# Measured TensorE and ScalarE durations in the build-time clock of a two-layer hybrid decoder kernel

## Chip, cores and metric

The kernel runs on one core of a Trainium2 chip as one program. The metric is the device time of one execution in microseconds (us), as the median over executions. The engines of the core are named as in the profile: PE (TensorE matmuls), PEld (its weight loads), DVE (VectorE), ACT (ScalarE), POOL (GpSimd) and SP (SyncE, which issues the DMAs here).

## What is computed

Two layers, each of three sub-layers in a row: a SwiGLU feed-forward network (FFN) at half weight, a token mixer, and a second such FFN. Each sub-layer is wrapped in RMS norms before and after it and in a shift, a scale and a gate that come from a conditioning vector `c`. The sequence has 256 rows, the model 1024 columns, the FFN 2816; all data are float32.

```python
def swiglu(h, w_in, w_out):
    gate, up = jnp.split(h @ w_in, 2, axis=-1)
    return (jax.nn.silu(gate) * up) @ w_out

def token_mixer(h, ...):
    proj = h @ w_in
    u, q, k, v, f, g_a, g_b = jnp.split(proj, cuts, axis=-1)
    y_ssm = s5_ssm(u, a_re, a_im, log_dt, b_re, b_im, c_re, c_im, d_skip)
    z_val, z_gate = jnp.split(jax.nn.gelu(y_ssm) @ glu_w, 2, axis=-1)
    y_a = z_val * jax.nn.sigmoid(z_gate)
    attn = forgetting_attention(q.reshape(shp), k.reshape(shp), v.reshape(shp), f + forget_b)
    y_b = attn @ attn_w_out
    merged = jax.nn.sigmoid(g_a) * y_a + jax.nn.sigmoid(g_b) * y_b
    return merged @ w_out

def reference(...):
    for l in range(DEPTH):
        mod = (jax.nn.silu(c) @ mod_w[l] + mod_b[l]).reshape(bsz, N_SUB, 3, D_MODEL)
        def pre(x_in, i):
            return rms_norm(x_in, norm_pre[l, i]) * (1.0 + mod[:, i, 1]) + mod[:, i, 0]
        def post_add(x_in, y, i, res_w):
            return x_in + res_w * mod[:, i, 2] * rms_norm(y, norm_post[l, i])
        x = post_add(x, swiglu(pre(x, 0), ffn_w_in[l, 0], ffn_w_out[l, 0]), 0, FFN_RES)
        y = token_mixer(pre(x, 1), ...)
        x = post_add(x, y, 1, 1.0)
        x = post_add(x, swiglu(pre(x, 2), ffn_w_in[l, 1], ffn_w_out[l, 1]), 2, FFN_RES)
    return x
```

`s5_ssm` is a diagonal state-space model with complex states (32 groups of 16 channels, 64 states each), and `forgetting_attention` is causal softmax attention with 8 heads of 64 and a bias that is a running sum of log-sigmoids.

## The kernel before

**Weights.** All weights come as one stream of pieces of 128 x 1024 float32, in an order worked out ahead. A product is made of three matmuls in the float32r type, of a high and a low part of both operands: `hi` with `xh`, `hi` with `xl`, `lo` with `xh`. So each piece goes through four steps: a DMA into a tile `raw`, a copy on ACT into `hi`, a subtraction on DVE into `lo`, and matmuls on PE. A piece of the modulation weights (`mod_w`) goes through a DMA and one DVE instruction (`raw<-raw,crow`), which sums into a column of `mc`; when the eight pieces of a vector are in, it is put to use, and after three gates PE transposes their columns (`gT`) so that they can be laid out as rows.

**Rows in two halves.** The 256 rows are two halves of 128. At a sub-layer's end, a half goes from its product `y` through `yg` (times a row of gates), `x` (added to the stream), `xn` (normalised), the PE transposes `xt<-kc,xn`, ACT's `xh<-xt,mc` and DVE's `xl<-xt,mc,xh`, and is then input to the next sub-layer. While the second half passes this chain, PE does the next sub-layer's first products for the first half alone: `n` in an FFN (natural orientation, turned around later with `hn`), `v` and `ga0` in a mixer. The function `pre_split` (line 555) issues the transposes of a half, and `hook` (line 1877) decides at which matmul.

**A mixer.** In this order PE does `v` and `ga0` (half of the first gate), `q`, `k`, `u`, then `ga1`, `gb0`, `gb1` (the rest of the gates). Each takes four pieces; `gb0_0` to `gb0_3` are the four pieces of `gb0`, and so on. Between them stand the attention: `sc<-kt,qt` (scores), on DVE `lg<-nbd,cq,sc` and `st<-lg` (bias, maximum), on ACT the exponentials `lg<-lg,st`, on PE the transposes `sc<-kc,lg`, on ACT their copy `lg<-sc`, on PE `sc<-lg,v` (values), then `ath` and `atl`, the parts of the result. `nbd` are masks of the bias. The state-space branch has tables that depend on the parameters alone (`pw`, `wc`, `ws`, `wt`: powers; `bt`, `bpr`, `bpi`: input matrices; `bT`, `D`, `cd`: transposed tables and the direct term) and work on data: `U` (copies of `u`), `vr`/`vi` on PE, products and scans on DVE that end in `zr` and `zi`, on PE `ys<-U,d` and `ys<-zr,c`. Behind them come `yb` (attention output, times the gate into `gb`), the copies `yg<-g` in pairs of one on DVE and one on ACT, `ygh` and `ygl` (parts of the branch's result), `z`, the merge `mt` and `ym` (the mixer's output).

**What sets the order.** The program is straight-line: the order of instructions is made when it is built. Each engine call goes through `Timed`, which tells a `Plan` what was issued; the plan keeps a clock for each engine, adds what `cost` (line 183) gives, and knows so when each tile would be ready. The PE's instructions are issued by plain loops; everything else waits in generators (`Task`, `Part`) with ranks. After each PE instruction `pace` lets `pick` (line 223) issue what could start by the PE's clock:

```python
            at = max(at, self.clk[eng])
            if t.rank <= 0:
                soon[eng] = min(at, soon.get(eng, at))
            elif soon.get(eng, 1e9) < max(at, now) + HOLD:
                continue
            at = max(at, now)
            if at <= until and (best is None or at < best[0]):
                best = at, t
```

The order on DVE and ACT, the DMAs (a DMA is issued when a tile of the stream comes free), and some of PE's order follow from this. On PE it is `hook`, which issues transposes once the clock has passed the chain's end,

```python
            if not last and not (task.done and task.at <= self.plan.clk["pe"]):
                return
```

and in the mixer `fill`, `past` and `there`, which put weight matmuls between the steps of the attention and the state-space branch until these are ready by the clock. The clock is a number in the builder only; the chip waits on semaphores, so another order changes no result. The constants that go with the clock (`HOLD`, `TURN`, `SLACK`, `KEPT`, `TABLES` and others at the top of the file) stay as they are.

Of the kernel before, what the change touches and what calls it, by code (L numbers as in the profile page):

```python
# [10 lines left out]
F32R = mybir.dt.float32r  # L11
# [152 lines left out]
class Plan:  # L164
# [18 lines left out]
    def cost(self, eng, op, outs, aps):  # L183
        n = max(x.free_size() for x in (outs or aps))
        if eng == "pe":
            if op == "transpose":
                return 0.107
            r = aps[-1]
            c = r.free_size() / 2400
            return max(c, 0.107) if r.dtype == F32R else max(4 * c, 0.214)  # L190
        if eng == "dve":
            return 0.07 + n / 960
        if eng == "act":
            return (0.1 if len(aps) < 3 else 0.18) + n / 1200
        if eng == "pool":
            return 0.4 + n / 400
        return n * 4 * P / 360e3
# [1763 lines left out]
```

## Time and profile before

| | us |
|---|---|
| three executions | 1183.67, 1193.74, 1189.22 |
| their median | 1189.22 |
| the profiled execution | 1182.35 |
| span of its trace, first to last instruction | 1180.6 |
| mean granted PE clock | 0.992 |
| PE idle for `z` waiting for `ygh`, once | 4.8 |
| PE idle for `gT` waiting for `mc`, once | 2.8 |
| PE idle for `v` waiting for `xl`, three times in all | 3.1 |

The span is one execution on the chip; the profiled execution's own time has 1.75 us more, which lie outside the first and last instruction. Times in the trace are microseconds from the span's start. A row of the timeline has the start, the length, the engine, the line, the operation with out<-in, and, in brackets, how long the engine idled before it and what released it. PE is pipelined: a 512-column matmul is listed with 0.39 us, while the next starts 0.23 us after it.

### The profile page before, as it was taken

To read this page: it belongs to the slowest core of one execution; us is meant where nothing else is said; L and a number is where in the kernel's file an instruction comes from. 1 tells how busy PE (TensorE), PEld (TensorE's weight loads), DVE (VectorE), ACT (ScalarE), POOL (GpSimd) and SP (SyncE) were. 2 spreads that over 40 slices of the span, in tenths; PEclk is the share of its full clock that TensorE was granted. 3 is DMA by queue.
4 is the path that set the end of the run, shared out by engine and by line. 5 is a ranking of instruction groups with operands and counts; after the bars stand their busy time and mean duration, and the time that the engine had idled before them with its cause. 6 is when DMAs were issued, how large, how long until landed. Compare 5 with 4: busy or idle time off the path is not lost.

```text
span 1180.6 us, 19407 instructions
## 1 busy us (share of the span) xinstructions
PE 1140.6 (97%) x7488; PEld 1015.5 (86%) x7488; DVE 912.7 (77%) x1529; ACT 608.6 (52%) x943; POOL 36.2 (3%) x62
## 2 busy tenths in 40 slices
PE   8999999998998999999999999999999999999997
PEld 5999998796786779999979989987987887999995
DVE  6988987897998889999678878878448798855532
ACT  5653452685556564444364475356355756543421
POOL 1000000000000010000010000001000001000000
PEclk9999999998999999999999999999999999999999
DMA  9999887577887669999769398966645566765300
GB/s 361 408 367 407 301 286 267 187 257 236 339 306 249 224 235 390 360 376 381 246 214 355 127 330 284 373 248 237 227 127 179 180 212 216 284 224 204 126 19 36
DMA packets 99186, 306.50 MB, mean 260 GB/s; under 512 B 16373, under 2 KB 26133, under 8 KB 99094
## 3 DMA queue, kind: packets, MB, share of 16 engines
q1 hardware_dynamic: 99094, 305.27, 71.6%
q8 instruction: 58, 0.95, 0.3%
q14 instruction: 34, 0.28, 0.1%
HBM read 291.51 MB, written 13.71 MB: 259 GB/s over the span
## 4 chain that ended last, share of the span: by engine, by line
PE 86%; DVE 7%; ACT 3%; DMA 2%; issue 2%; POOL 1%; SPq 0%; DVEq 0%; POOLq 0%; ACTq 0%
PE f L128 35%; PE y L128 20%; PE n L128 5%; PE ym L128 3%; PE ga L128 3%; PE gb L128 3%; PE z L128 3%; PE k L128 2%; PE q L128 2%; PE v L128 2%; PE ys L128 2%; PE u L128 2%; ACT xh L128 1%; DVE raw L128 1%; PE yb L128 1%
## 5 line engine op out<-in xcount | busy, mean ns | idle before, releaser
L128 DVE TENSOR_TENSOR lo<-raw,hi 128x1024 fp32r<-128x1024 f32 x368 | 437.1, 1218 | 27.2 <-ACT hi L128 21.3
L128 ACT ACTIVATE hi<-raw 128x1024 fp32r<-128x1024 f32 x367 | 370.7, 1055 | 68.3 <-PE f L128 38.7
L128 PE MATMUL f<-xl,hi 128*128 128x256 f32 x1216 | 341.4, 281 | 2.7 <-DVE xl L128 2.7
L128 PE MATMUL f<-xh,hi 128*128 128x256 f32 x1216 | 342.0, 281 | 1.9 <-ACT xh L128 1.9
L128 PE MATMUL f<-xh,lo 128*128 128x256 f32 x1216 | 341.0, 280 | 0.0
L128 PEld LDWEIGHTS f<-xh,lo 128*128 128x128 f32 x1216 | 232.4, 191 | 0.0
L128 PEld LDWEIGHTS f<-xl,hi 128*128 128x128 f32 x1216 | 228.4, 188 | 4.6 <-DVE xl L128 3.6
L128 PEld LDWEIGHTS f<-xh,hi 128*128 128x128 f32 x1216 | 228.5, 188 | 3.8 <-ACT xh L128 2.5
L128 PE MATMUL y<-hi,ht 128*128 128x512 f32 x704 | 196.2, 391 | 0.8 <-DVE yg L128 0.8
L128 DVE SCALAR_TENSOR_TENSOR raw<-raw,crow 128x1024 f32<-128x1024 f32 x144 | 173.3, 1218 | 6.0 <-DMA raw<-ws 5.9
L128 PEld LDWEIGHTS y<-hi,ht 128*128 128x128 f32 x704 | 129.3, 188 | 26.2 <-DVE yg L128 1.1
L128 ACT ACTIVATE sg<-f 128x512 f32<-128x512 f32 x38 | 22.7, 597 | 222.7 <-PE f L128 215.4
L128 PE MATMUL y<-lo,ht 128*128 128x512 f32 x352 | 109.3, 390 | 0.8 <-ACT yg L128 0.8
L128 DVE TENSOR_TENSOR sg<-sg,f 128x512 f32<-128x512 f32 x38 | 26.1, 687 | 90.0 <-ACT sg L128 89.9
L128 PEld LDWEIGHTS y<-lo,ht 128*128 128x128 f32 x352 | 66.1, 188 | 15.1 <-ACT yg L128 1.2
L128 PE MATMUL n<-hi,xl 128*128 128x512 f32 x96 | 37.9, 395 | 1.7 <-DVE xl L128 1.7
L128 ACT ACTIVATE lg<-lg,st 128x128 f32<-128x128 f32 (+1 forms) x64 | 26.1, 444 | 25.3 <-DVE st L128 25.3
L128 PE MATMUL n<-hi,xh 128*128 128x512 f32 x96 | 38.4, 400 | 0.0
L128 PE MATMUL n<-lo,xh 128*128 128x512 f32 x96 | 37.7, 392 | 0.0
L128 DVE TENSOR_TENSOR yg<-y,row 128x1024 f32<-128x1024 f32 (+1 forms) x9 | 9.9, 1103 | 32.8 <-ACT xn L128 23.6
L128 DVE TENSOR_TENSOR ht<-sg,ht 128x512 fp32r<-128x512 f32 x38 | 26.1, 687 | 9.8 <-ACT ht L128 9.5
L128 ACT ACTIVATE xh<-xt,mc 128x128 fp32r<-128x128 f32 x80 | 21.7, 383 | 22.1 <-PE xt L128 22.1
(276 smaller groups left out, 1646.7 us busy)
## 6 DMA issues: line engine op xcount, KB each, us to landing
raw<-ws SPq DMA_DIRECT2D x512, 512.0 KB, 5.8
row<-sg SPq DMA_DIRECT2D x11, 512.0 KB, 8.0
sbt<-bT SPq DMA_DIRECT2D x8, 512.0 KB, 3.0
sc<-cd SPq DMA_DIRECT2D x16, 256.0 KB, 8.0
bt<-sbt SPq DMA_DIRECT2D x8, 512.0 KB, 4.5
c<-sc SPq DMA_DIRECT2D x8, 512.0 KB, 10.2
d<-sd SPq DMA_DIRECT2D x4, 512.0 KB, 4.6
w<-sw SPq DMA_DIRECT2D x4, 512.0 KB, 5.8
```

The costliest lines, as they stand in the source:

```text
L128: r = f(*a, **k)
```

## The change

The change is to the numbers in `Plan.cost` alone.

```diff
         if eng == "pe":
             if op == "transpose":
-                return 0.107
+                return 0.109
             r = aps[-1]
             c = r.free_size() / 2400
-            return max(c, 0.107) if r.dtype == F32R else max(4 * c, 0.214)
+            return c + 0.012 if r.dtype == F32R else max(4 * c, 0.224)
         if eng == "dve":
             return 0.07 + n / 960
         if eng == "act":
-            return (0.1 if len(aps) < 3 else 0.18) + n / 1200
+            return (0.19 if len(aps) < 3 else 0.27) + n / 1350
```

In the clock a 512-column float32r matmul now takes 0.225 us (0.213 before), one of 256 columns 0.119 (0.107), a small float32 one 0.224 (0.214), an ACT instruction on 1024 columns 0.949 (0.953) and one on 128 columns 0.285 (0.207). DVE's numbers stay: 1.137 us for 1024 columns. PE's clock so runs 6 to 11% slower against DVE's. The instructions are the same ones, on every engine; their order differs from the first pieces of the first FFN on.

PE, the start of the second FFN of layer 0, where `n` is made for the first half and the transposes of the second half come in. Before (`hi_4394` and `lo_4464` are the third piece, `hi_4404` and `lo_4495` the fourth):

```order
L128 MATMUL n_668_4504<-hi_4386,xl 128x512
L128 MATMUL n_668_4504<-hi_4394,xh 128x512
L128 MATMUL n_668_4504<-lo_4464,xh 128x512
...
L128 MATMUL n_668_4504<-hi_4394,xl 128x512
L128 MATMUL xt_4531<-kc,xn_635_4335 128x128 x8
L128 MATMUL n_668_4504<-hi_4404,xh 128x512
```

And now (`hi_4393` and `lo_4476` are the third piece):

```order
L128 MATMUL n_669_4506<-hi_4382,xl 128x512
L128 MATMUL xt_4525<-kc,xn_635_4335 128x128 x8
L128 MATMUL n_669_4506<-hi_4393,xh 128x512
L128 MATMUL n_669_4506<-lo_4476,xh 128x512
L128 MATMUL n_669_4506<-hi_4393,xl 128x512
...
L128 MATMUL n_669_4506<-hi_4402,xh 128x512
```

The eight transposes have moved ahead of the six matmuls of the third piece (three kinds, each for two blocks of 128 input columns; `hook` is called after each piece). The same move is made at five places: at the start of three FFNs like this one (the second of layer 0 and both of layer 1) and at the starts of both mixers, among the pieces of `ga0`. The first half's transposes move at one place only, at the start of the layer-0 mixer, from behind the last piece of the FFN to twelve matmuls ahead of that.

DVE, the layer-0 mixer around the first softmax. Before (`lo_3359` is the split of piece `ga1_2`):

```order
L128 TENSOR_TENSOR nbd_451_3110<-nbd_451_3110,cm 128x1024
L128 COPY U_3281<-u_3063 32x4x64
L128 SCALAR_TENSOR_TENSOR lg_3292<-nbd_449_3108,cq_3051,sc_3282 128x128
...
L128 TENSOR_REDUCE st_3293<-lg_3292 128x2 x2
L128 TENSOR_SCALAR st_3293<-st_3293 128x4
L128 COPY U_3281<-u_3063 32x4x64
L128 TENSOR_TENSOR wt_3237<-ws_3236,pw_3238 128x32
L128 TENSOR_TENSOR pw_3238<-pw_3238 128x16 x2
L128 TENSOR_TENSOR ws_3236<-wc_3235,pw_3238 128x16x2
L128 TENSOR_TENSOR pw_3238<-pw_3238 128x16 x2
L128 TENSOR_TENSOR lo_3359<-raw_424_2950,hi_3343 128x1024
```

And now (`lo_3427` is the split of piece `ga1_3`, `lo_3441` that of `gb0_0`):

```order
L128 TENSOR_TENSOR wt_3097<-ws_3096,pw_3098 128x512
L128 TENSOR_TENSOR wc_3095<-wc_3095,wt_3097 128x16x32
L128 COPY U_3339<-u_3179 32x4x64
L128 TENSOR_TENSOR nbd_461_3224<-nbp_3225,cm 128x1024
L128 TENSOR_TENSOR nbd_463_3226<-nbd_463_3226,cm 128x1024
L128 SCALAR_TENSOR_TENSOR lg_3350<-nbd_461_3224,cq_3177,sc_3340 128x128
...
L128 TENSOR_REDUCE st_3351<-lg_3350 128x2 x2
L128 TENSOR_SCALAR st_3351<-st_3351 128x4
L128 TENSOR_TENSOR lo_3427<-raw_419_2891,hi_3403 128x1024
L128 RECIPROCAL st_3351<-st_3351 128x4
L128 TENSOR_TENSOR lo_3441<-raw_422_2907,hi_3410 128x1024
```

The powers (`pw`, `wc`, `ws`, `wt`) were at 32 columns at this point and are now at 512, their last; the split of `ga1_2` now stands ahead of `nbd`, and the first split behind the softmax rows is that of the next piece, `ga1_3`. On PE `ga1_3` and `gb0_0` now stand ahead of the first transposes `sc<-kc,lg`, where they stood behind the state-space products `vr` and `vi`; all of `yb` for the first half stands ahead of `ys<-zr,c`, which had `yb` between its parts. On DVE the last two `gb<-gb,yb`, which follow the last `yb`, now stand ahead of all eight copies `yg<-g` of the branch's second half; three of these stood ahead of them.

PE, the end of the layer-0 mixer's `z`. Before:

```order
L128 MATMUL z_4173<-hi_4053,ygh_3871 128x512 x2
L128 MATMUL z_4173<-lo_4086,ygh_3871 128x512 x2
L128 MATMUL z_4173<-hi_4053,ygl_3872 128x512 x2
L128 MATMUL gT_4247<-kc,mc 24x128
L128 MATMUL ym_626_4256<-hi_4066,xh 128x512 x2
```

And now:

```order
L128 MATMUL z_4007<-hi_4038,ygh_3913 128x512 x2
L128 MATMUL z_4007<-lo_4058,ygh_3913 128x512 x2
L128 MATMUL z_4007<-hi_4038,ygl_3914 128x512 x2
L128 MATMUL gT_4146<-kc,mc 24x128
L128 MATMUL z_4151<-hi_4050,ygh_3913 128x512 x2
```

The transpose `gT` stood behind all of `z`, ahead of `ym`; it now stands in the middle of `z`, ahead of the second group of output columns. Its last modulation pieces on DVE stood behind `z` and now stand ahead of it.

In the layer-1 mixer, PE's first `ys<-zr,c` moves ahead of the last `sc<-lg,v` and the first piece of `yb`, and on ACT the copy `lg<-sc` of the third softmax moves ahead of one `hi`. In the FFNs the splits, the modulation pieces and the DMAs shift by some rows against PE.

## Prediction

> **What bounds the kernel now.** I read the page's busy shares first, then busy time by stage, then the waits of the tensor engine (PE), then the timeline at each long wait.
>
> ```profile
> span 1180.6 us, 19407 instructions
> PE 1140.6 (97%) x7488; PEld 1015.5 (86%) x7488; DVE 912.7 (77%) x1529; ACT 608.6 (52%) x943; POOL 36.2 (3%) x62
> ```
>
> ```profile
> 183.00:206.00 23.00, 23.00 (x108) 19.03 (x106) 17.13 (x23) 8.36 (x11) 1.59 (x4) 1.00 0.78 282
> 206.00:222.00 16.00, 13.29 (x60) 10.36 (x60) 11.02 (x18) 11.64 (x27) 2.35 (x4) 1.00 0.44 148
> 222.00:276.00 54.00, 54.00 (x463) 49.96 (x461) 50.59 (x107) 37.02 (x67) 0.00 (x0) 1.00 0.71 244
> 276.00:316.00 40.00, 33.73 (x200) 26.92 (x200) 33.45 (x117) 23.98 (x60) 1.16 (x2) 0.91 0.80 280
> 316.00:361.00 45.00, 42.74 (x260) 35.68 (x259) 41.31 (x58) 26.46 (x45) 0.00 (x0) 1.00 0.85 321
> 361.00:394.00 33.00, 25.41 (x110) 20.43 (x109) 30.12 (x43) 21.09 (x28) 0.00 (x0) 0.95 0.75 247
> 394.00:430.00 36.00, 35.95 (x169) 28.98 (x167) 29.43 (x36) 19.02 (x36) 5.55 (x8) 1.00 0.62 211
> 430.00:605.00 175.00, 174.25 (x1190) 161.42 (x1190) 147.45 (x204) 81.18 (x101) 2.36 (x4) 1.00 0.88 333
> ```
>
> The windows are cut where stages end (`u` of the layer-0 mixer at 276). The columns are window, length, then busy time and instructions of PE, weight load, VectorE (DVE), ScalarE (ACT), GpSimd, then granted PE clock, DMA share and GB/s. PE is busy 1140.6 of 1180.6 us, so an order of instructions cannot win more than some tens of us. In an FFN (430 to 605) it idles 0.75 us of 175: nothing is to be won there. The layer-0 mixer, 276 to 394, leaves 6.3 + 2.3 + 7.6 = 16 us idle, and DVE is busy 104.9 of those 118 us: that stretch runs at DVE's pace as much as at PE's. What is decided there decides the time.
>
> ```profile
> 280.00:287.00 7.00, 3.29 (x14) 2.17 (x12) 6.76 (x22) 4.66 (x15) 1.16 (x2) 0.90 0.59 176
> 287.00:294.00 7.00, 6.04 (x21) 4.63 (x23) 4.83 (x32) 4.14 (x7) 0.00 (x0) 0.62 0.69 228
> 367.00:374.00 7.00, 2.72 (x6) 2.15 (x7) 6.91 (x9) 6.06 (x8) 0.00 (x0) 0.78 0.86 268
> 905.00:910.00 5.00, 3.63 (x18) 2.82 (x19) 4.89 (x10) 2.38 (x3) 0.00 (x0) 0.68 0.61 211
> ```
>
> Here the granted clock falls behind waits. The lost clock is 7 x 0.10 + 7 x 0.38 = 3.4 us, 7 x 0.22 = 1.5 and 5 x 0.32 = 1.6: about 1.6 us for each cut, two of them around 287.
>
> **The change, part by part.** No instruction is added or removed, so all costs are waits. In the FFNs the order of weight splits shifts by a few rows; PE has no wait there and the splits keep their lead: 0, with 0 to +1 as bounds. The head, where PE waits for DVE,
>
> ```profile
> PE f L128 <- DVE xl L128: 2.7, 4, 0.9
> ```
>
> keeps DVE's rows but for swaps of neighbours: 0, and no more than one such wait of 0.9 either way.
>
> *Second-half transposes.* The transposes `xt` of rows 128 to 255 go six 512-column matmuls earlier at five places. One of them:
>
> ```profile
> 613.49 1.28 DVE L128 SCALAR_TENSOR_TENSOR xn<-x,ssx,row 128x1024 f32<-128x1024 f32 x1 [0.75 <-POOL ssx L128]
> ...
> 614.83 1.09 PE L128 MATMUL xt<-kc,xn 128*128 128x128 f32 x8
> ...
> 616.47 0.39 PE L128 MATMUL n<-hi,xh 128*128 128x512 f32 x1
> 616.70 0.39 PE L128 MATMUL n<-lo,xh 128*128 128x512 f32 x1
> ...
> 617.62 0.40 PE L128 MATMUL n<-lo,xh 128*128 128x512 f32 x1
> 618.58 0.50 PE L128 MATMUL n<-hi,xl 128*128 128x512 f32 x1 [0.56 <-DVE xl L128]
> ```
>
> ```profile
> PE n L128 <- DVE xl L128: 1.7, 3, 0.6
> ```
>
> `xn` ends at 614.77 and the transposes start 0.06 us behind it. In the new order DVE has the same rows ahead of `x` and `xn` (only the product `yg` goes ahead of one split, and `x` comes right where it came), so `xn` ends when it did, and PE meets the transposes 6 x 0.23 = 1.36 us too early. It gets back the wait behind them: 618.58 - 617.62 is 0.96 against a pitch of 0.23, so 0.73, and about 0.1 for the slower start after a wait. Net 1.36 - 0.84 = +0.52, three times by the row of waits; at the layer-1 mixer that wait is longer,
>
> ```profile
> 812.97 0.50 PE L128 MATMUL v<-hi,xl 128*128 128x512 f32 x1 [0.80 <-DVE xl L128]
> ```
>
> and +0.3 is left. Together +1.9; bounds 0 (if `xn` comes earlier with `yg`) and 4 x 1.36 = +5.4. The fifth place is the next part.
>
> *Boundary into the layer-0 mixer.* The first transposes go twelve matmuls (2.7 us) earlier, which hides a wait of 1.46 us behind them:
>
> ```profile
> 208.73 0.50 PE L128 MATMUL v<-hi,xl 128*128 128x512 f32 x1 [1.46 <-DVE xl L128]
> ```
>
> In their place eight table products of the state-space branch (0.3 to 1 us each) stand on DVE ahead of the splits of the third and fourth value pieces. Laid end to end from `xl`, DVE ends these splits at about 210.0 and 212.4, where PE wants them at 208.9 and 211.6; then `ga0_1` waits some 1.3 us. About 3 us of new waits against 1.9 + 1.1 us of old ones: 0, bounds -1.9 and +1.9.
>
> *Layer-0 mixer.* When `u` ends (276.0) DVE has done 6.4 us more of rows than before (the powers of the state matrix, less three modulation pieces and a split). DVE idled 5.9 + 5.0 + 3.4 = 14.3 us from 183 to 276, so these fit. Then:
>
> ```profile
> 277.68 1.20 DVE L128 TENSOR_TENSOR nbd<-nbp,cm 128x1024 f32<-128x1024 f32 x1
> ...
> 281.82 0.35 DVE L128 SCALAR_TENSOR_TENSOR lg<-nbd,cq,sc 128x128 f32<-128x128 f32 x1
> ...
> 283.38 1.00 DVE L128 TENSOR_REDUCE st<-lg 128x2 f32<-128x256 f32 x2
> ...
> 284.10 0.50 PE L128 MATMUL ga<-hi,xh 128*128 128x512 f32 x1 [1.43 <-ACT hi L128]
> ...
> 285.61 1.22 DVE L128 TENSOR_TENSOR lo<-raw,hi 128x1024 fp32r<-128x1024 f32 x1
> ...
> 286.88 0.79 PE L128 MATMUL ga<-lo,xh 128*128 128x512 f32 x1 [2.28 <-DVE lo L128]
> ```
>
> Before, `ga1_2` waits 1.43 + 2.28 us, since its split stands behind the softmax rows. Now its split comes ahead of them, and `ga1_3`, which PE meets next, takes its place. Ahead of the split of `ga1_3` DVE has, from 276: two `nbd` and two copies of `U` (281.82 - 277.68 = 4.1 us), two more copies and four table rows (by their columns, 1024 taking 1.2: 2 x 0.3 + 4 x 0.6 = 3.0), two splits (2.4), six `lg` (283.38 - 281.82 = 1.6), `st` (1.1) and itself (1.2): 13.4, so 289.4. PE, which would have begun `ga1_2` at about 284.1 - 1.5 = 282.6 and needs 12 x 0.23 = 2.7 us for it, is there at 285.3 and waits 4.1 us, with a clock cut behind it as at 287. I walked on in this way, DVE's rows laid end to end and PE's beside them. The softmax parts are now parted by weight pieces on PE, so that the smaller waits mostly go: of the 6.3 + 2.3 us idle until 361, 3.7 are those of `ga1_2` and some 4 of the rest. With the 3.4 us of clock PE wins 11 and pays 4.1: 7 us ahead. But DVE, which by then has been busy without a break, takes back half: the split of `gb1_3` comes 1.4 us late, and the first product of `yb` waits about 3 us, its `atl` standing behind two scan products; 1 us of old waits goes there. So `yb` ends about 3.5 us earlier. Then the second half of `z`:
>
> ```profile
> 361.40 1.28 DVE L128 SCALAR_TENSOR_TENSOR gb<-gb,yb 128x512 f32<-128x512 f32 x2
> ...
> 370.61 0.61 ACT L128 ACTIVATE ygh<-yg 128x512 fp32r<-128x512 f32 x1
> ...
> 371.28 1.22 PE L128 MATMUL z<-hi,ygh 128*128 128x512 f32 x2 [4.79 <-ACT ygh L128]
> ...
> 393.00 0.27 PE L128 MATMUL gT<-kc,mc 128*24 128x128 f32 x1 [2.81 <-DVE mc L128]
> ```
>
> Before, `ygh` starts 9.2 us after the `gb` products that follow `yb`, three of its eight copies on DVE, each in turn with one on ACT, being done ahead of them. Now all eight come behind, which at about 0.8 a pair makes 11.6. So `z` goes on 3.5 - 2.4 = 1.1 us earlier than at 371.3, after a wait of some 7 us that takes in the clock cut as before. The row transpose `gT` stands where its modulation rows are long done, so 2.8 us go. With +0.5 for a later `xl` and +1.5 for the clock cut behind `ga1_3`: -1.1 - 2.8 + 0.5 + 1.5 = -1.9. Bounds: all the idle time of 276 to 394 gone, -16; nothing gained and the 6.4 us of DVE rows late, +6.4. I take the walk's value, since the rows that make it are in the trace.
>
> *Layer-1 mixer.*
>
> ```profile
> 899.82 0.18 DVE L128 RECIPROCAL st<-st 128x4 f32<-128x4 f32 x1 [0.90 <-ACT lg L128]
> ...
> 906.37 1.21 PE L128 MATMUL sc<-lg,v 128*64 128x128 f32 x12 [1.85 <-ACT lg L128]
> ...
> 912.86 1.50 ACT L128 ACTIVATE lg<-lg,st 128x128 f32<-128x128 f32 x4
> ...
> 914.35 0.82 PE L128 MATMUL sc<-kc,lg 128*128 128x128 f32 x6
> ...
> 918.61 0.88 PE L128 MATMUL sc<-lg,v 128*64 128x128 f32 x12
> 918.85 1.22 DVE L128 TENSOR_TENSOR zr<-zr,t 128x1024 f32<-128x1024 f32 x1
> ```
>
> ACT's copy `lg<-sc` goes ahead of one split, so the wait of 1.85 shrinks by a split's 1.2, and the clock cut behind it (1.6) may go. But the next softmax, ready at 912.86 + 1.50 = 914.36, comes from DVE at its old time, and PE used it at 914.35: it now waits there for the 2.8 us it won. Behind that, `ys<-zr` stands ahead of the values; DVE saves the idle 0.90 at two reciprocals and ends `zr` 1.8 us earlier, about when PE comes; `atl`, behind copies of `yg`, costs some 0.5. Net +0.5, bounds -2.8 (both gains kept) and +2.5.
>
> Sum: +1.9 + 0 - 1.9 + 0.5 = +0.5 us on the profiled execution's 1182.35 us, so 1182.8. That execution lies 6.9 us under the median 1189.22 of the three runs shown; against the median the sum gives 1189.7 us.
>
> [...] By the rows, a wait of 1.85 us (906.37) was followed by a cut clock, one of 1.46 (208.73) was not (1.00 in 206 to 222), nor one of 2.81 (393.00; 1.00 in 394 to 430). [...]
>
> **The rivals.**
> Faster: DVE's rows pack better than in my walk, and of the 16 us idle and 5 us of lost clock in the layer-0 mixer half goes, 10.5 in place of 1.9: 1181; if all but 3 go, 1174. For it speaks that DVE has 13 us idle in 276 to 394; against it, that most of the waits there end on DVE's own chain of scans, products and copies, which grows no shorter.
> Slower, by the clock: the new waits of 1.4 to 1.6 us at four transposes, and those of about 3 us in both mixers, are each followed by a cut of 1.6: 6 x 1.6 = +9.6, 1199. It decides whether 1.6 us suffices; the rows leave that open between 1.46 and 1.85.
> Slower, by DVE: if the 6.4 us of earlier rows are not absorbed, the softmax and all behind it come that much later: +6.4, 1196; it decides if less than half of DVE's 14.3 idle us before 276 can be used, because rows stand behind one that waits.
> No effect at all, if the new numbers gave the old order, is excluded by the pieces of order shown above; its time would be 1189.
>
> **How the numbers follow.** Forecast 0.58, faster rival 0.18, clock 0.14, DVE 0.10. A measurement of this kernel can tell about 1% from no change, so the bounds are 1177.3 and 1201.1. Faster by over 1%: most of the faster rival and a tail of the forecast, 0.17. Slower: the slower rivals where both act or where the upper bounds of the transposes join them, 0.12. Within 1%: 0.71. The range, 1175 to 1199, takes in both slower rivals' values and most of the faster one's.
>
> **What would show it.** In the profile after: waits of `xt` for `xn` of about 1.5 us at four places and none of `n` for `xl` behind; no wait at `gT`; `ga<-lo` of about 4 us near 285 and `z<-ygh` of 7 us near 362; the wait at 906 small and one of 3 us before the next softmax transposes. The prediction is wrong if the FFNs get waits, if `f` waits longer for `xl` in the head, if `u` ends late because DVE's earlier rows did not fit, or if the clock is cut behind waits of 1.5 us.

## The result, and the profile after

The changed kernel takes 1224.43 us (median of 4 executions, 1221.38 to 1225.74), the kernel before on the same chip 1186.45 us: ratio 1.031, 95% interval 1.025 to 1.037. It is slower by about 3%, and the forecast was no change. The profiled execution took 1223.9 us. Its page begins, and has as busy time of the engines:

```profile
span 1222.1 us, 19426 instructions
...
PE 1160.6 (95%) x7488; PEld 1034.8 (85%) x7488; DVE 913.9 (75%) x1529; ACT 608.9 (50%) x943; POOL 34.7 (3%) x62
```

DVE and ACT have the work that they had, to 0.2%. PE has the same 7488 matmuls, yet was busy 20.0 us longer (1160.6 against 1140.6): they ran at a lower clock (0.971 granted in the mean over the execution, against 0.992). The other 21.5 us of the 41.5 are idle time. Where these arose is seen when both spans are cut at the same places in the work: the first matmul `n` of the second feed-forward (FFN) of layer 0, the first matmul of layer 1's `q`, and the first `n` of layer 1's second FFN. Windows of before and then of after; the columns are window, length, busy time and instructions of PE, PEld, DVE, ACT and POOL, granted PE clock, DMA share and GB/s:

```profile
0.00:417.10 417.10, 392.13 (x2556) 342.32 (x2557) 358.08 (x707) 234.85 (x383) 13.43 (x27) 0.99 0.83 300
417.10:826.40 409.30, 406.45 (x2725) 368.09 (x2724) 342.42 (x533) 210.56 (x305) 14.30 (x20) 1.00 0.80 297
826.40:985.00 158.60, 155.12 (x972) 134.62 (x971) 107.06 (x167) 87.16 (x157) 3.52 (x6) 0.99 0.58 191
985.00:1180.60 195.60, 186.90 (x1242) 170.51 (x1240) 105.16 (x125) 76.00 (x100) 4.95 (x9) 0.99 0.43 152
```

```profile
0.00:448.10 448.10, 406.62 (x2555) 355.24 (x2556) 359.26 (x707) 234.38 (x382) 15.23 (x27) 0.94 0.76 280
448.10:859.30 411.20, 405.67 (x2725) 367.82 (x2724) 342.25 (x534) 210.98 (x305) 11.81 (x20) 1.00 0.79 295
859.30:1026.20 166.90, 161.73 (x971) 141.17 (x970) 107.42 (x167) 86.85 (x156) 3.52 (x6) 0.95 0.52 182
1026.20:1222.10 195.90, 186.57 (x1242) 170.58 (x1240) 104.96 (x126) 76.67 (x100) 4.12 (x9) 0.99 0.43 151
```

The first stretch loses 31.0 us: idle time (length less PE's busy time) goes from 25.0 to 41.5, and busy time for the same matmuls from 392.1 to 406.6. The second, which is nearly all FFN, loses 1.9. The third, layer 1's mixer from `q` on, loses 8.3, of which 6.6 are busy time, the clock being 0.95 in place of 0.99. The last loses 0.3.

The 31.0 split further. The first transposes `xt` of layer 0's mixer begin 0.8 us later with twelve 512-column matmuls (2.7 us) fewer done, so 3.5 us were lost in the first FFN. When `u` begins the lag is 5.2 us (268.2 against 263.0), with 32 `D` matmuls more behind it; 16 of these took 0.66 us in a row, so the lag for the same work is 3.9, and the entry into the mixer cost 0.4. The other 27 us arise from `u` on in layer 0's mixer.

The 3.5 us at the head are a cut clock. Windows of before and of after:

```profile
20.00:30.00 10.00, 9.10 (x77) 8.91 (x78) 9.86 (x18) 6.47 (x11) 0.00 (x0) 1.00 1.03 406
```

```profile
20.00:30.00 10.00, 8.04 (x47) 7.84 (x48) 9.86 (x18) 6.25 (x10) 0.00 (x0) 0.66 1.03 408
```

PE's waits for `xl` are no longer in sum (2.5 us, before 2.7), but 1.96 of them now come in one piece, right behind a wait of 1.87 for `xh`, and the clock falls to 0.66: 47 matmuls in ten microseconds in place of 77. (In executions of kernels with the same start, below, `xt` begins between 203.0 and 205.9, so this part varies by some 3 us; before's own wait of 1.87 for `xh`, with one of 0.81 for `xl` behind it, left the clock at 1.00.)

**Layer 0's mixer.** The timeline of after, with what each instruction waited for in brackets:

```profile
290.99 2.95 ACT L128 ACTIVATE hi<-raw 128x1024 fp32r<-128x1024 f32 x3 [3.81 <-DMA snb<-cumt]
...
292.10 0.50 PE L128 MATMUL ga<-hi,xh 128*128 128x512 f32 x1 [2.28 <-ACT hi L128]
...
295.03 1.23 DVE L128 TENSOR_TENSOR nbd<-nbp,cm 128x1024 f32<-128x1024 f32 x1 [7.25 <-DMA nbp<-snb]
...
297.35 1.23 DVE L128 TENSOR_TENSOR nbd<-nbd,cm 128x1024 f32<-128x1024 f32 x1 [1.09 <-DMA nbd<-snb]
...
302.59 0.80 PE L128 MATMUL ga<-lo,xh 128*128 128x512 f32 x1 [9.99 <-DVE lo L128]
...
316.99 0.42 DVE L128 TENSOR_TENSOR atl<-sc,ath 128x256 fp32r<-128x256 f32 x1
...
317.51 0.66 PE L128 MATMUL vi<-U,bt 128*128 128x64 f32 x2 [3.53 <-issue]
```

PE stands 9.99 us before `ga1_3`'s `lo` matmuls. Its split is queued on DVE behind the masks `nbd`, and DVE itself stands 7.25 us for the transfer `nbp<-snb`. SP, which issues that transfer in its order, tells why. SP's issues in after, then in before (start, length of the issuing, what, how many):

```profile
267.05 12.56 SPq L128 DMA_DIRECT2D sd<-kt  x16
279.65 2.13 SPq L128 DMA_DIRECT2D bt<-sbt  x4
281.95 1.16 SPq L128 DMA_DIRECT2D d<-sd  x2
283.15 0.61 SPq L128 DMA_DIRECT2D snb<-cumt  x1
291.03 0.33 SPq L128 DMA_DIRECT2D nbp<-snb  x1
```

```profile
268.28 0.32 SPq L128 DMA_DIRECT2D snb<-cumt  x1
272.41 0.33 SPq L128 DMA_DIRECT2D nbp<-snb  x1
...
275.82 12.75 SPq L128 DMA_DIRECT2D sd<-kt  x16
288.62 1.86 SPq L128 DMA_DIRECT2D bt<-sbt  x4
```

In after, the state-space tables are done by the builder's clock before `u` is begun, since `D`'s last 32 matmuls have moved ahead; so their 16 stores `sd` and the loads `bt` and `d` go to SP ahead of `snb`. From `snb` to `nbp`, which needs it in memory, it then takes 7.9 us in place of 4.1, with the loads of `bt` and `d` under way. The masks are issued 18.6 us later than before, while `u` is only 5.2 us later.

The second stand, 3.53 us between the first `vr` and the first `vi` product, bears the releaser "issue": the profile sees no data that `vi` waits for. `atl` on DVE ends at 317.41 and `vi` starts at 317.51; `atl` reads the PSUM tile that `vi` is to overwrite, and now stands behind the six `lg` and the `st` of the next softmax. What follows it costs more than the stand. Windows of after:

```profile
318.00:326.00 8.00, 8.00 (x39) 8.00 (x39) 6.22 (x10) 2.48 (x9) 2.03 (x2) 0.50 1.03 408
326.00:334.00 8.00, 8.00 (x35) 7.61 (x35) 0.00 (x0) 1.65 (x2) 0.00 (x0) 0.50 0.94 358
334.00:342.00 8.00, 8.00 (x46) 5.79 (x46) 6.37 (x12) 1.44 (x3) 0.00 (x0) 0.97 0.30 101
```

PE is busy every moment from 318 to 334, at a clock of 0.50: a pair of `vr` and `vi` products (128x64, float32, each listed as two matmuls) takes 0.86 us, against 0.45 in before.

**Layer 1's mixer.** PE at the next softmax transposes, and the windows behind:

```profile
947.62 0.33 PE L128 MATMUL sc<-kc,lg 128*128 128x128 f32 x1 [2.54 <-ACT lg L128]
```

```profile
947.00:952.00 5.00, 4.02 (x21) 3.75 (x21) 4.97 (x6) 4.84 (x8) 0.00 (x0) 0.69 0.08 34
952.00:960.00 8.00, 8.00 (x39) 8.00 (x39) 5.44 (x5) 1.43 (x2) 0.00 (x0) 0.50 0.00 1
960.00:964.00 4.00, 4.00 (x26) 3.76 (x25) 0.52 (x2) 0.60 (x1) 0.00 (x0) 0.50 0.07 11
```

The same picture: a stand of 2.54 us, and then the narrow `ys` products run at 0.50 for some 14 us.

### The profile page after: what moved, and what is told of

It is laid out like the page before. It is cut to its first block, busy times and chain, and to the rows that moved or that the text cites. A ratio compares the mean times of both kernels' runs of the same rounds, so it can differ in the third digit from the quotient of the medians.

```text
span 1222.1 us, 19426 instructions
## 1 busy us (share of the span) xinstructions
PE 1160.6 (95%) x7488; PEld 1034.8 (85%) x7488; DVE 913.9 (75%) x1529; ACT 608.9 (50%) x943; POOL 34.7 (3%) x62
## 4 chain that ended last, share of the span: by engine, by line
PE 59%; DVE 4%; ACT 2%; issue 1%; POOL 1%; DMA 1%; DVEq 0%; POOLq 0%; ACTq 0%
PE f L128 25%; PE y L128 13%; PE n L128 4%; PE z L128 3%; PE ym L128 3%; PE ga L128 2%; PE ys L128 1%; PE gb L128 1%; PE yb L128 1%; PE u L128 1%; PE q L128 1%; PE k L128 1%; POOL ssx L128 1%; ACT xh L128 1%; PE xt L128 1%
## 5 line engine op out<-in xcount | busy, mean ns | idle before, releaser
L128 PE MATMUL ga<-lo,xh 128*128 128x512 f32 x64 | 26.3, 411 | 11.3 <-DVE lo L128 11.3
```

What stands on the lines that cost most here:

```text
L128: r = f(*a, **k)
```

## The experiments

Ratios are against the kernel before, run on the same chip; a difference to the changed kernel is one of medians (1224.4). The changed kernel was measured against other executions of before (1186.45), so such a difference is good to some 3 us only: by the ratios the gains of experiments 1, 2, 3, 6 and 7 are about 5, 4, 4, 4 and 23 us, and the intervals of the first four overlap the changed kernel's. What each edit does at its place is read from the traces.

**1. The three issues on another queue.** On the changed kernel, `snb`, `nbp` and `nbd` are issued by GpSimd (`side`):

```diff
+        self.side = Timed(plan, "dma", nc.gpsimd)
...
-        nc.sync.dma_start(row, ct[0:16, 0:P])
+        nc.side.dma_start(row, ct[0:16, 0:P])
...
-        nc.sync.dma_start(self.nb[1], flat[0:1, :].to_broadcast([P, D]))
-        nc.sync.dma_start(self.nb[2], flat[1:2, :].to_broadcast([P, D]))
+        nc.side.dma_start(self.nb[1], flat[0:1, :].to_broadcast([P, D]))
+        nc.side.dma_start(self.nb[2], flat[1:2, :].to_broadcast([P, D]))
```

> Of the changed kernel, with the three small transfers of the forget rows (snb<-cumt, nbp<-snb, nbd<-snb) issued from GpSimd's queue in place of SyncE's; every other instruction stays where it is. Theory (SyncE's queue): the masks came late because their transfers stand behind sixteen sd<-kt, four bt<-sbt and two d<-sd on one in-order queue. Then DVE's wait of 7.25 us of nbd for nbp shrinks to under 1.5, PE's wait of 9.99 us of ga for lo to 2 to 4, and the time falls by 7 to 13 us from 1224, to 1211 to 1217. Rival (DVE is too full of early table rows): the masks come in time but DVE does not, the wait of ga stays over 8 us, and the time stays within 3 us of 1224.

1217.73 us, ratio 1.0265 (1.0228 to 1.0303): 6.7 us less. The timeline has `snb` on GpSimd, and PE at the same split:

```profile
271.27 0.76 POOL L128 DMA_DIRECT2D snb<-cumt  x1 [55.69 <-DMA sd<-kt]
273.95 0.57 POOL L128 DMA_DIRECT2D nbp<-snb  x1 [1.91 <-DMA sd<-kt]
```

```profile
291.34 0.50 PE L128 MATMUL ga<-lo,xh 128*128 128x512 f32 x1 [4.13 <-DVE lo L128]
```

`nbp` is issued 17 us earlier than in after (`u` begins 2.2 earlier), and the stand of 9.99 us is 4.13. At the first `n` of the second FFN the lag on before is 19.3 us, 11.7 less than in after; 2.2 of these were there when `u` began, ahead of the first moved transfer, so 9.5 us are from the edit on. In the two FFNs that follow 4.5 us are lost again (415.7 us in place of 411.2), where a wait of 2.31 us of `gT`, up to 766.85, is followed by a clock of 0.83; experiment 7 has the same edit without this loss, so what brought it is not shown. That SP's order cost some 9 us in layer 0's mixer is shown, with an uncertainty of some 3: the same stretch, from `u` to the second FFN, takes 179.9 us in after and 182.5 in experiment 3, which changes nothing there.

**2. `atl` ahead of the next scores.** On the changed kernel, layer 0 alone:

```diff
-        self.values(0, sc)
+        value = self.values(0, sc)
+        if l == 0:
+            self.finish(value)
         sc = self.scores(1, qt, kt)
```

> Of the changed kernel, with the two instructions that read the first value tile (ath, atl) of the layer-0 mixer put ahead of the next scores, so that atl on DVE stands ahead of the six lg rows in place of behind them. Theory (a PSUM tile held by atl, and a clock that stays cut): vi's wait of 3.5 us, which the profile calls issue, goes, since vi writes the PSUM tile that atl reads last; with it goes the cut clock of 318 to 331, in which 32 pairs of narrow products run at half speed: -3.5 - 6.6 = -10 us, 1214. First rival: the wait goes but the clock is cut anyway by the wait of 10 us before: -3.5, 1221. Second rival: vi waits for something else (the transfer of bt, PE's own instructions): no change, 1224.

1219.19 us, ratio 1.0279 (1.0240 to 1.0318): 5.2 less. The stand before `vi` shrinks to 1.93 us, and the trace now names `atl` as its releaser, which bears out the reading of "issue" above. But the clock is cut all the same: the first products run at 1.00 (316 to 320), and from about 320.5 the rest at half (0.55 in 320 to 326, 0.50 in 326 to 334). So the shorter stand did not save the clock. At the 13th `vr` this kernel lags as after does (26.2 and 26.5 us); the 5.8 us that it has won at the second FFN (lag 25.2 in place of 31.0) come at later waits.

**3. Layer 1's stand filled.** On the changed kernel, 24 extra 256-column matmuls, whose result is overwritten, ahead of the softmax transposes at 947:

```diff
-        self.probs_t(nxt)
+        self.probs_t(nxt, 24 if l else 0)
...
+        for i in range(heat):
+            nc.raw.tensor.matmul(ps[:, 0:256], self.xh[:, 0, 0, :], self.xh[:, :, 0, :], start=True, stop=True)
```

> Of the changed kernel, with 24 dummy 256-column matmuls on PE (2.8 us by their pitch of 0.118) in the wait of 2.5 us ahead of the last softmax transposes of the layer-1 mixer; they write columns that the transposes overwrite. Theory (a cut clock stays cut under narrow matmuls): the clock stays 1.00 from 947 to 968, where it was 0.50 to 0.75, the products ys run at 0.22 us a pair in place of 0.43, and 5 to 8 us are saved: 1217. Rival (the narrow matmuls pull the clock down themselves, or another bound stands behind them): the clock is still cut or PE waits as long elsewhere, and the time is within 2 us of 1224.

1218.35 us, ratio 1.0274 (1.0221 to 1.0326): 6.1 less, with more work on PE. Windows of this kernel at that place:

```profile
947.00:955.00 8.00, 7.75 (x64) 7.26 (x62) 7.40 (x11) 6.79 (x16) 0.00 (x0) 1.00 0.35 131
955.00:963.00 8.00, 7.72 (x67) 7.08 (x66) 7.84 (x14) 4.37 (x9) 0.00 (x0) 1.00 0.27 100
```

The clock stays at 1.00, and 131 matmuls (24 of them the extra ones) are done in 16 us, where after has 86 in the 17 us shown above. Layer 1's mixer, from `q` to the FFN, takes 159.4 us in place of 166.9, and 158.6 in before: nearly all of its 8.3 us was the clock behind that one stand.

**4. TensorE's numbers alone.** ScalarE's are the old ones:

```diff
-            return (0.19 if len(aps) < 3 else 0.27) + n / 1350
+            return (0.1 if len(aps) < 3 else 0.18) + n / 1200
```

> Of the change, TensorE's durations alone; ScalarE's as before. The order of SyncE's queue at the layer-0 mixer is that of the whole change (sd, bt and d ahead of snb). Theory (it is this order that costs, and it comes from TensorE's numbers): 1215 to 1230. Rival (the two sets of numbers cost together, or ScalarE's alone): within 1% of before, 1175 to 1198.

1200.62 us, ratio 1.014 (1.009 to 1.019), between the two expectations. SP's order is that of after, and PE stands 5.76 us before `ga1_3`; yet up to the second FFN it lags by only 4.3 us. `vi` waits 0.39 us, the clock stays at 1.00 through the narrow `vr` and `vi` (314 to 326), and two stands of before (4.8 us at `z`, 2.8 at `gT`) are gone. Its loss is in the two FFNs, 421.1 us against 409.3. SP's order alone does not make the loss.

**5. ScalarE's numbers alone.** On the kernel before:

```diff
-            return (0.1 if len(aps) < 3 else 0.18) + n / 1200
+            return (0.19 if len(aps) < 3 else 0.27) + n / 1350
```

> The kernel before with ScalarE's new durations alone; the build then orders SyncE's queue as before (snb, nbp, nbd ahead of the sd loads) and has the first atl ahead of the next six lg rows. Theory (the loss hangs on SyncE's order and on atl's place, which TensorE's new numbers set, alone or with ScalarE's): 1183 to 1196 us, and no wait over 4 us ahead of the last ga panel of layer 0. Rival (the two sets of numbers add up, each with its own loss: 1224 less the 1201 of TensorE's numbers alone leaves about 23 us for ScalarE's): 1203 to 1212 us.

1194.56 us, ratio 1.0064 (1.0034 to 1.0094). The time is as the theory had it; that no wait over 4 us would be left was wrong: PE stands 5.6 us before `ga`'s split, and 6.2 for `gT`, and loses 6.2 us up to the second FFN and 5.4 in layer 1's mixer. The two sets apart cost about 17 and 8 us (1.4% of 1184 and 0.64% of 1188), 24 in sum; together they cost 38.

**6. Layer 0's stand filled.** On the changed kernel, 28 extra matmuls behind the first `vr` product; `atl` stays late:

```diff
                 mm(o[:, 64 * j:64 * j + 64], bt[c][j // 8][:, sl(j)], u[:, 64 * j:64 * j + 64], start=True, stop=True)
+                for i in range(28 if l == j == c == 0 else 0):
+                    nc.raw.tensor.matmul(vr[:, 512:768], self.xh[:, 0, 0, :], self.xh[:, :, 0, :], start=True, stop=True)
```

> The changed kernel with 28 extra 256-column matmuls on TensorE behind layer 0's first vr product, where it stands 3.5 us for atl; atl stays late. Theory (the stand sets the clock to 0.50 and the narrow vr and vi products, though TensorE is then busy without a break, don't bring it back): with the stand filled these products run at 1.00, 0.45 us each in place of 0.86, and about 8 us go: 1214 to 1219 us. Rival (the 10 us wait ahead of it, or the narrow products themselves, set the clock): it stays at 0.50 from 318 to 334 us, and the time is 1224 to 1228 us.

1219.41 us, ratio 1.0280 (1.0221 to 1.0339): 5.0 less. Windows of this kernel from the stand on:

```profile
315.90:320.00 4.10, 4.10 (x36) 3.98 (x34) 4.03 (x14) 1.55 (x6) 0.00 (x0) 1.00 1.03 416
320.00:326.00 6.00, 6.00 (x56) 6.00 (x56) 5.52 (x9) 2.53 (x9) 1.57 (x2) 1.00 1.02 406
```

56 matmuls in 6 us at a clock of 1.00, where after had 39 in 8. The stand of 9.55 us ahead of `ga1_3` is still there, so neither it nor the narrow products by themselves cut the clock at these products, which is 1.00 from 315.9 to 326. The time falls by 5 us and not by 8: in the traced execution, the slowest of the four (1223.5), the lag at the second FFN is still 27.8 us (31.0 in after).

**7. Edits 1, 2 and 3 together.**

> The changed kernel with the three single edits together: snb, nbp, nbd on GpSimd's queue, atl ahead of the next scores in layer 0, 24 extra matmuls in layer 1's stand. Theory (three separate losses): their single gains add up, 6.7 + 5.2 + 6.1 = 18 us off 1224.4, so 1206 us, and down to 1200 us if the 5.8 us that the first edit gave back in the second feed-forward do not come; range 1199 to 1208. Rival (one loss seen three times: a wait that is taken away comes back at the next place): 1213 to 1219 us.

1199.61 us, ratio 1.0118 (1.0055 to 1.0180): 24.8 us less, and the loss of the first edit in the FFNs does not come (411.5 us). So the three losses are separate; none comes back when another is taken away. 1.2% stays: up to the second FFN this kernel still lags by 14.4 us, with idle time 2.3 us over before and busy time 12.1 over it. `atl` still makes `vi` wait 2.0 us, and the clock falls to 0.50 behind that.

**8. The kernel before with edit 1.**

> The kernel before with snb, nbp, nbd on GpSimd's queue. Theory (before, SyncE issues them as soon as cumt is there, so the queue costs nothing): 1181 to 1187 us, the wait of 2.3 us ahead of ga's last panel as it was. Rival (the queue cost the kernel before something too, since weight loads stand behind these three issues): 1176 to 1180 us.

1185.29 us, ratio 0.9993 (0.9964 to 1.0021): no difference, as expected. So the queue cost something in layer 0's mixer of after, where the `sd` stores and the `bt` and `d` loads stood ahead of these issues (some 9 us, experiment 1), and nothing that shows in before, where they did not.

**9. The one decision in the kernel before.** With the old numbers, the tables' task is finished ahead of `u`:

```diff
+        if l == 0:
+            self.finish(self.tables)
         if self.tables.done and not self.bt:
```

> The kernel before, with its old durations, and one line added: in layer 0 the tables' task is finished ahead of u's product. This alone puts D's remaining 32 matmuls and the sd, bt and d transfers ahead of snb on SyncE and the first atl behind the next six lg rows on VectorE, as the changed kernel has them. Theory (this one decision carries the loss of layer 0's mixer; the new durations only tip it): layer 0's mixer as in the changed kernel, with the stand of about 10 us ahead of ga's last panel and that of 3.5 us between vr and vi, and layer 1 as before: 1205 to 1216 us. Rival (the loss comes from many small moves of the two sets of durations, as TensorE's alone, with the same order on SyncE, lost nothing in layer 0's mixer): 1184 to 1196 us.

1208.47 us, ratio 1.0177 (1.0107 to 1.0248). SP's issues, and the windows of the first and the third stretch:

```profile
276.99 10.99 SPq L128 DMA_DIRECT2D sd<-kt  x16
288.02 1.86 SPq L128 DMA_DIRECT2D bt<-sbt  x4
...
290.95 0.44 SPq L128 DMA_DIRECT2D snb<-cumt  x1
299.47 0.33 SPq L128 DMA_DIRECT2D nbp<-snb  x1
```

```profile
0.00:442.20 442.20, 410.41 (x2556) 358.08 (x2557) 358.02 (x707) 234.00 (x383) 13.49 (x27) 0.94 0.78 283
...
851.70:1009.90 158.20, 153.98 (x971) 133.44 (x970) 106.98 (x167) 87.16 (x157) 3.52 (x6) 1.00 0.57 195
```

This line alone brings 25.1 us up to the second FFN. 6.2 of them are there when `u` begins: 1.3 us are 32 more `D` matmuls (0.66 for 16, above) and 2.9 waits for `cd`; the other 2 were not taken apart (over the whole stretch the clock is 0.94, in before 0.99). The other 18.9 come from `u` on, where SP's order and `atl`'s place are after's: `vi` stands 3.17 us, and the clock is 0.50 behind it. Layer 1's mixer loses nothing. The stand before `ga`'s last panel was expected at 10 us and is 1.0; `gb` waits 4.0 and `sc` 4.5 us in its place, since more pieces stand ahead of the masks. So the theory holds for the total and for `vi`, not for the place of each wait. Experiment 4 has the same order on SP and lost little in this mixer, so that order does not cost by itself. That the clock at the narrow products makes the difference is not shown: experiment 6 keeps it at 1.00 there and still lags by 27.8 us.

**10. Wide matmuls amid the narrow ones.** On the changed kernel 40 extra 256-column matmuls, by the loop of experiment 6, behind the fourth pair of `vr` and `vi`; the stand stays.

> The changed kernel with 40 extra 256-column matmuls behind the fourth pair of vr and vi products of layer 0, after the stand for atl, which stays. Theory (narrow products hold the clock down, wide ones bring it back): 0.50 when the extra matmuls begin, 1.00 at their end or within 2 us of it, and the remaining 56 products at 0.45 us each. Rival (after a stand the clock stays at 0.50 for a fixed 16 us, whatever runs): 0.50 until about 334 us, and products of 0.86 us behind the extra ones. The time itself should be 1221 to 1228 us by either and tells little.

1225.38 us, one execution. Windows of this kernel:

```profile
312.00:316.00 4.00, 0.82 (x7) 0.71 (x7) 3.93 (x14) 1.37 (x6) 0.00 (x0) 1.00 1.03 415
316.00:318.00 2.00, 2.00 (x12) 2.00 (x12) 1.52 (x3) 1.76 (x7) 0.00 (x0) 0.59 1.04 414
318.00:320.00 2.00, 2.00 (x12) 2.00 (x12) 2.00 (x5) 0.69 (x2) 1.47 (x1) 0.55 1.03 406
320.00:330.00 10.00, 10.00 (x88) 9.92 (x87) 2.67 (x4) 0.32 (x1) 0.57 (x2) 1.00 1.03 408
```

The extra matmuls start at 317.6; some two microseconds on the clock is back at 1.00, and the narrow products behind them keep it. So no fixed time of 16 us ran after this stand: in after the narrow products, with PE busy without a break, did not raise the clock from 0.50 in 16 us, and here it stays at 1.00 under them.

**11. New numbers from layer 0's second FFN on.** Until the end of layer 0's mixer the old ones are in force, and the order there is before's:

```diff
+        self.old = True
...
+            if self.old:
+                return max(c, 0.107) if r.dtype == F32R else max(4 * c, 0.214)
...
         self.merged = merges[1]
+        self.plan.old = False
```

> The changed kernel, with the old durations in force until the end of layer 0's mixer and the new ones from there on; up to that point the order is the one of before. Theory (31 of the 41 us arise up to the end of layer 0's mixer, 2 in the feed-forwards behind it, 8 in layer 1's mixer): about 10 us over before, 1191 to 1198 us. Rival (what layer 1 loses hangs on how layer 0 left the queues and the clock of the build): 1183 to 1189 us.

1200.67 us, ratio 1.0084 (1.0040 to 1.0128): by the ratio 10 us over before, as expected, while the median lies above its range. In the traced execution layer 1's mixer takes 166.90 us, the 8.3 over before that it takes in after. The executions lie far apart, from 1187.7 to 1206.7, and the traced one (1206.5) shows a loss of 10.8 us up to the second FFN, in the order of before:

```profile
295.98 0.41 PE L128 MATMUL vi<-U,bt 128*128 128x64 f32 x2 [1.66 <-DMA bt<-sbt]
```

```profile
302.00:310.00 8.00, 8.00 (x39) 8.00 (x39) 3.88 (x8) 0.85 (x1) 0.00 (x0) 0.50 0.80 305
```

The first `vi` waits 1.66 us for `bt`, and the narrow products run at 0.50. In the profiled execution of before `bt` was in time, though SP issued it no earlier (288.6 there, 288.7 here): PE began `vr` at 295.49 there and at 293.88 here, so PE was early. A second cut stands behind `gT`, which waits as in before, with the same matmuls behind it; there the clock stayed at 1.00:

```profile
402.38 0.37 PE L128 MATMUL gT<-kc,mc 128*24 128x128 f32 x1 [2.82 <-DVE mc L128]
```

```profile
402.00:405.00 3.00, 2.62 (x7) 2.19 (x8) 2.37 (x6) 0.56 (x1) 0.00 (x0) 0.51 0.12 45
```

**12. `bt` ahead of `sd`.** On the kernel before, the four `bt` loads are issued ahead of the 16 `sd` stores, and no other engine's order changes:

```diff
...
+        if self.s == 1:
+            self.bt = self.load_bt()
         self.s5_place(l, kt)
```

> The kernel before with one move on SyncE: the four bt loads of a mixer are issued ahead of the 16 sd stores in place of behind them, some 12 us earlier; no other engine's order changes. Theory (the kernel before runs between 1180 and 1195 us because bt lands only just ahead of the first vr and vi products, and where it comes 1.7 us late the narrow products behind it run at 0.50, as in the profiled execution of the kernel with the new durations from the second feed-forward on): no stand between vr and vi in any execution, so the slow end goes: median 1180 to 1185 us, highest under 1189 us. Rival (the spread of before arises elsewhere): median 1184 to 1190 us, and a range as wide as before's.

1184.90 us (1182.02 to 1186.43, 12 executions), before 1184.13 (1180.54 to 1195.53, 17): ratio 0.9996 (0.9970 to 1.0022). The spread falls from 15 to 4 us, which speaks for `bt`'s landing as what makes the slow end of it; the median does not move. Experiment 8 agrees: its trace has `bt` issued at 283.1, 5.5 us earlier than before, and its ten executions lie within 6 us. No execution of before at the long end was traced, so this stays short of shown. The traced execution starts `vr` 2.3 us earlier than before, runs all of `vr` and `vi` at 1.00, and loses the clock amid the next narrow products, `ys`. PE idles 0.65 us in 340 to 350, and the clock there is 0.72. Before idles the same, 0.64 us, ahead of the same products and keeps 1.00, so the wait alone does not explain the fall. Windows of experiment 12, then of before at the same matmuls:

```profile
340.00:350.00 10.00, 9.35 (x50) 8.25 (x48) 9.99 (x14) 3.85 (x8) 0.00 (x0) 0.72 0.65 230
350.00:360.00 10.00, 10.00 (x42) 9.14 (x42) 1.44 (x6) 4.20 (x7) 0.00 (x0) 0.60 0.54 203
```

```profile
342.00:352.00 10.00, 9.36 (x71) 8.49 (x70) 10.00 (x13) 4.28 (x8) 0.00 (x0) 1.00 0.73 263
```

No kernel that ran is faster than before; this one is as fast, and steadier.

## Why the prediction was wrong

*FFNs and second-half transposes: right.* Three stretches of transposes were to cost 0.52 us each; from the first `n` to the first `f` the lag grows by 0.4 us at each of the three FFN entries (31.0 to 31.4, 31.4 to 31.8, 41.2 to 41.6). PE waits 1.31 to 1.33 us for `xn`, where 1.36 was worked out.

*Head: wrong in size.* One more wait of at most 0.9 either way was allowed. The waits only moved together, and the clock that fell there was not priced: 3.5 us in this execution, of a part that varies by some 3.

*Boundary: right*, 0.4 within its bounds of 1.9; `ga0_1` waits 1.26 us, where 1.3 was worked out.

*Layer 0's mixer: the failed step.* -1.9 was predicted, +27 came, over the upper bound of +6.4. Two things were left out of the walk.

First, it laid DVE's rows end to end and took the masks' transfers as being there, as they were before. SP's queue was not walked, though `D`'s matmuls were seen to move and the tables' 22 transfers hang on them. With that one omission taken away, in experiment 1, the stand before `ga1_3` is 4.13 us, where the walk had 4.1. And DVE was not held up by its earlier rows: ahead of the masks it stood idle 7.25 us for a DMA.

Second, a cut of the clock was priced at 1.6 us, from places where wide matmuls follow it. The stand at 302.59 is such a place: behind it the matmuls come at a pitch of 0.43 us until 307, and at 0.23 from there, so it costs 2.2 us. At the 64-column products of after the cut lasted as long as these did, 16 us at 0.50, and cost 8. That `atl` would be late was seen, but for `yb`; that the PSUM tile of `vi` hangs on it was not.

One step was right: the wait of `gT` is gone. The wait for `ygh` is 2.94 us and not 7.

*Layer 1's mixer: mechanism right, size wrong.* The wait of 1.85 us shrinks to 1.10, and the next softmax waits 2.54, where 2.8 was worked out. The term that was mis-sized is the clock behind it, for which nothing was put in: 6.6 us, shown by experiment 3.

*The rivals.* The slower one by the clock had the right kind of mechanism and the wrong places: behind the waits at the transposes (1.3 us, wide matmuls behind them) the clock stayed at 1.00, and the two before narrow products cost 8 and 6.6 us, not 1.6. *Which waits were followed by a cut:* 2.54 us in after, 1.93 in experiment 2 and 1.66 in experiment 11 were; those of 1.3 at the transposes and of 2.81 at `gT` in before were not. Under wide matmuls the clock was back at 1.00 some 2 us on in experiment 10 and 4.4 behind the stand at 302.59; under the narrow ones it stayed at 0.50 through 16 us of unbroken work.

*What is settled.* One decision of the builder, tables done before `u`, carries most of the loss: from `u` to the second FFN before takes 154.1 us, before with this decision 173.0 (experiment 9) and after 179.9. Its parts in after are SP's order (some 9 us there), `atl`'s place (5.8 up to the second FFN) and the clock held down by narrow products; layer 1's loss is the clock behind one stand. *What stays open:* why experiment 4, with the same order on SP, escapes most of it; the 14 us up to the second FFN that experiment 7 leaves are for the most part busy time at a lower clock, but were not taken apart further; and why TensorE's numbers alone lose 12 us in the FFNs: in that trace PE waits there 7.4 us for `xn` at four groups of transposes (4.3 at five in after) and 2.0 at `D`, but no experiment took these away.

## What to carry to other kernels

When an order changes, walk the queue that issues the transfers too, and ask of each table or task that is done sooner what it now issues ahead of whom. Price a wait of PE by what follows it: where the clock fell behind it, it cost here itself and 1.5 us (371.28 in before) to 3.5 (the head of after) ahead of matmuls of 256 and 512 columns, and itself and 8 us (`vr` and `vi`) or 6.6 (`ys` in layer 1) ahead of runs of 16 and 14 us of narrow float32 ones. Whether the clock falls could not be told from the wait alone (2.8 us at `gT`: 1.00 in before, 0.51 in experiment 11). A clock in a builder that knows durations, but neither how long transfers are issued nor PE's own clock, does not give a better order because some of its durations are better.

## What the runs showed of the hardware

Narrow products (128x64, float32) did not raise PE's clock in after, however densely they followed one another: PE was busy for all of 318 to 334 at 0.50. In experiment 10 the clock was back at 1.00 within about 2 us of 40 wide ones (256 columns, float32r), and stayed there through the rest of the narrow ones. Width and type change together there, so which of the two counts is not shown. Waits of 1.66 and 1.93 us ahead of such a run were followed by a cut in experiments 11 and 2. But the length of a wait and what follows it did not decide alone: the wait of 2.8 us at `gT` left the clock at 1.00 in before and was followed by 0.51 in experiment 11, and one of 0.64 us at `ys` left it at 1.00 in before, while experiment 12, idle for 0.65 there, shows 0.72. What else decides stays open. So layer 0's narrow `vr` and `vi` ran at two speeds with the same order of instructions, 1.00 in before and 0.50 in experiment 11; the 15 us of spread in the kernel before, 4 in experiment 12, fit this.
